# A hybrid attention and recurrence backbone on one core: the product of two norm vectors moves into the tile they are loaded into, and the pool of constants becomes 32 bytes shorter

## The chip, the core and the metric

The kernel runs on one core of a Trainium2 chip. A core has five engines that work side by side: TensorE (PE, with its weight loads shown apart as PEld), VectorE (DVE), ScalarE (ACT), GpSimd (POOL) and SyncE (SP). Here SP and POOL issue the DMAs. The metric is the device time of one execution in microseconds (us). The time before is the median of three runs.

## The reference

Two layers work on 1024 latent tokens of width 1024 (a raster 64 wide) with 256 context tokens before them. Layer 0 projects to neighbourhood attention with 16 heads and to a bidirectional mLSTM with 4 heads; layer 1 is a bidirectional gated linear attention (HGRN2) with 16 heads. Each has one input and one output projection. Cut to what the change touches:

```python
x, ctx: (1, 1024, 1024), (1, 256, 1024)            # float32 throughout
shift, scale, gate = split(silu(c) @ w_ada[l] + b_ada[l])
h = rms(x, norm_w[l]) * (1 + scale) + shift          # same for ctx
# layer 0
qa, ka, va, za, qb, kb, vb, ob, zb, g = split(h @ w_in_ab)
qa = rms(heads(qa, 16), q_norm)                      # q_norm, k_norm: 64 numbers each
ka = rms(heads(ka, 16), k_norm)
oa = softmax(qa * 64**-0.5 @ ka.T + bias) @ va       # neighbourhood 8 x 16, and the context
hb = mlstm_bidir(qb, kb, vb, gates)
x = x + gate * (concat(oa * silu(za), rms(hb * sigmoid(ob)) * silu(zb)) @ w_out_ab)
# layer 1
q, f_fwd, f_bwd, i, z = split(h @ w_in_c)
x = x + gate * ((rms(gla_bidir(silu(q), i, f)) * silu(z)) @ w_out_c)
```

Since a score is the product of a normed query and a normed key, the kernel multiplies q_norm, k_norm and 64**-0.5 = 0.125 into one vector, and applies it to the keys alone.

## The kernel before

**Precision.** The big products are done in three matmuls. A float32 operand is split into a high part, rounded to the matmul's own format (`fp32r` in the profile), and a low part, the rest: `split` (L73 on ACT, L74 on DVE). `dense` (L129, L130, L131) then adds high by high, high by low and low by high; `out_part` does the same for output projections (L858, L859, L860). In the names, `wh` and `wl` are a weight's two parts, `hh` and `hl` those of the modulated input h, `yh` and `yl` those of the mixers' output, `woh` and `wol` those of an output weight, `wzh` and `wzl` those of a weight of layer 1 that serves the value and gate columns. Smaller products (attention, recurrences, transposes) are plain float32.

Each matmul has a stationary operand, loaded into the array first (PEld), and a moving one, streamed through it. `proj_nat` has h stationary and a weight moving (256 or 512 columns); `proj_tr` has the weight stationary and h moving. In the profile's names the moving operand stands first.

**Stages.** Up to some 300 us: conditioning, norm and modulation of the input into `hh`, `hl`. Then layer 0 to about 1640 us: the attention (`na`), with the mLSTM's projections as filler between its steps, then the mLSTM's recurrence (`ml`), again with projections between. Then layer 0's output projection and layer 1's input (to about 1840 us), the 16 heads of layer 1 (`hg`, 88 us each), and from about 3290 us the last output projection, with blocks named w to w6 in the code.

**Order.** The order on each engine is set when the program is built, by a scheduler that works through the code and through priorities (`filler`, `urgent`). All waits are semaphores.

**Memory.** SBUF tiles have an address within a partition; each takes a multiple of 32 bytes. Pools of tiles grow from the left or, with `side="right"`, from the right end. The first pool on the left is the pool of constants, `const` (`cp` in the code, L1165), which starts at 16512. It holds ident (512 bytes), mhalf (32), ab0 and ab1 (128 each), cT and normw (64 each), badap (128), hnb (32), hnc (64), qkn (32), qknp (32), bg (32), lbc (128), sct (64), lb (128) and lbm (64): 1632 bytes, so that the next pool starts at 18144. All other pools on the left stand behind it: the weights of layer 0 (`w0`), the tiles of attention and recurrences (`na`, `ml`, `hg`), layer 1's wz, and the last projection's weights w3 to w6 (`wl1`). On the right stand a tile of 32 bytes (`edge`), then `hh` and `hl`, the weights of layer 1 (`w1`) and the y tiles of the last projection (`oy`).

The function that the diff touches is `build`; the lines that count are L1197 to L1201, where `qkn` is loaded by a DMA on POOL's queue and DVE makes the product `qknp`. That product is read by the attention's key preparation (`akh`, L686, and `akl`, L687).

Of the kernel before, what the change touches and what calls it, by code (L numbers as in the profile page):

```python
# [10 lines left out]
F32 = mybir.dt.float32  # L11
# [8 lines left out]
P = 128  # L20
# [25 lines left out]
class Prog:  # L46
# [1114 lines left out]
    def build(self):  # L1161
        tc, nc, a = self.tc, self.nc, self.a
        dma = nc.sync.dma_start
        with ExitStack() as es:
            cp = es.enter_context(tc.tile_pool(name="const", bufs=1))  # L1165
# [21 lines left out]
            def load(name, shape, eng=nc.gpsimd):  # L1187
                t = self.t(cp, shape, F32, name)
                eng.dma_start(out=t, in_=a[name])
                return t  # L1190
# [3 lines left out]
            self.badap = load("badap", [P, 2, 16])  # L1194
            self.hnb = load("hnb", [P, KD])
            self.hnc = load("hnc", [P, 16])
            qkn = load("qkn", [P, 2])  # L1197
            self.qkn = self.t(cp, [P, 1], F32, "qknp")
            nc.vector.tensor_scalar(
                out=self.qkn, in0=qkn[:, 0:1], scalar1=qkn[:, 1:2], scalar2=0.125, op0=ALU.mult, op1=ALU.mult  # L1200
            )  # L1201
# [10 lines left out]
            for i in range(2):  # L1212
# [6 lines left out]
                out=self.lb[:, 1, :], in0=self.lb[:, 0, :], scalar1=-1.0, scalar2=1.0, op0=ALU.mult, op1=ALU.add  # L1219
# [405 lines left out]
```

## Time and profile before

| | |
|---|---|
| median of three runs | 3446.57 us (3445.27 to 3448.31) |
| profiled execution | 3444.31 us |
| its span, first to last instruction | 3442.5 us |
| granted TensorE clock, mean | 0.992 |
| PE, PEld busy | 3368.1 us (98%), 2972.1 us (86%) |
| DVE, ACT, POOL busy | 2051.4, 1407.0, 664.0 us |
| DMA | 333.56 MB, mean 97 GB/s |

Busy time is the union of an engine's instructions. PE's matmuls overlap in a pipeline and their ends are modelled, so the pace of PE is read from the starts of matmuls that follow each other, not from their durations. Rows of a stage table give, for a stretch of time, the busy time of PE, PEld, DVE, ACT and POOL with the number of instructions, the granted clock (1.00 is full), the busy share of the DMA engines and GB/s. A row of a group gives line, engine, operation, names (out<-in), shape and count, then busy us, mean ns of one, and idle time ahead of it with what ended it. A row in order of time gives start and duration in us.

### The profile page before, as it was taken

What the parts mean: (1) busy time and instruction counts of PE and PEld (TensorE: products, weight loads), DVE (VectorE), ACT (ScalarE), POOL (GpSimd) and SP (SyncE); (2) the same over time, 40 slices, a digit from 0 to 9 for tenths busy, and PEclk for the clock granted to TensorE, in tenths of its full rate; (3) what the DMA queues carried; (4) which work ended last, traced back from release to release, by engine and by line L of the source; (5) the groups of instructions that cost most, each with busy time, mean ns of one, the idle gap of its engine ahead of it and who ended that gap; (6) DMA issues with size and microseconds to landing.
All of it is one profiled execution on the core that took longest, in us unless ns stands there. A gap on an engine that the chain in (4) does not pass through costs nothing.

```text
span 3442.5 us, 64358 instructions
## 1 busy us (share of the span) xinstructions
PE 3368.1 (98%) x25044; PEld 2972.1 (86%) x25044; DVE 2051.4 (60%) x4786; ACT 1407.0 (41%) x3310; POOL 664.0 (19%) x1036
## 2 busy tenths in 40 slices
PE   7999999999999999999999999999999999999988
PEld 5689999888989888898888999989999988889866
DVE  5336666566655466777666555555555555555657
ACT  5235544455444444454354333333333333333432
POOL 2121222122211111221100111111111111121023
PEclk9999999999999999999999999999999999999999
DMA  6522222232233443444652111111111111111364
GB/s 242 214 75 70 79 77 74 76 90 83 68 90 99 144 125 121 127 132 144 218 166 71 50 58 55 58 59 58 57 59 59 50 50 50 54 59 37 119 204 151
DMA packets 327152, 333.56 MB, mean 97 GB/s; under 512 B 30696, under 2 KB 277672, under 8 KB 324800
## 3 DMA queue, kind: packets, MB, share of 16 engines
q1 hardware_dynamic: 287808, 222.76, 21.8%
q0 software_dynamic: 39040, 106.69, 8.8%
q8 instruction: 197, 3.23, 0.4%
q14 instruction: 107, 0.88, 0.1%
HBM read 259.40 MB, written 69.79 MB: 96 GB/s over the span
## 4 chain that ended last, share of the span: by engine, by line
PE 87%; DMA 4%; issue 3%; DVE 3%; ACT 1%; POOL 1%; SPq 0%; POOLq 0%; DVEq 0%; ACTq 0%
PE mm L129 19%; PE mm L131 19%; PE mm L130 19%; PE s L1021 4%; PE acc L798 2%; PE tr L778 2%; PE mm L858 2%; PE mm L859 2%; PE mm L860 2%; PE s L579 2%; PE acc L570 2%; PE acc L560 1%; PE acc L1097 1%; PE tr L1033 1%; PE acc L1098 1%
## 5 line engine op out<-in xcount | busy, mean ns | idle before, releaser
L131 PE MATMUL mm<-hh,wl 128*128 128x512 f32 (+1 forms) x1600 | 584.2, 365 | 0.0
L129 PE MATMUL mm<-hh,wh 128*128 128x512 f32 (+1 forms) x1600 | 584.1, 365 | 0.0
L130 PE MATMUL mm<-hl,wh 128*128 128x512 f32 (+1 forms) x1600 | 583.6, 365 | 0.0
L129 PE MATMUL mm<-wh,hh 128*128 128x256 f32 (+1 forms) x1520 | 473.6, 312 | 1.7 <-ACT ev L314 1.0
L131 PE MATMUL mm<-wh,hl 128*128 128x256 f32 (+1 forms) x1520 | 470.1, 310 | 0.3 <-DVE hl L273 0.3
L130 PE MATMUL mm<-wl,hh 128*128 128x256 f32 (+1 forms) x1520 | 470.3, 309 | 0.0
L131 PEld LDWEIGHTS mm<-hh,wl 128*128 128x128 f32 x1600 | 301.6, 189 | 46.0 <-issue 0.3
L129 PEld LDWEIGHTS mm<-hh,wh 128*128 128x128 f32 x1600 | 301.9, 189 | 45.3 <-issue 0.8
L130 PEld LDWEIGHTS mm<-hl,wh 128*128 128x128 f32 x1600 | 301.8, 189 | 43.4 <-issue 0.2
L129 PEld LDWEIGHTS mm<-wh,hh 128*128 128x128 f32 x1520 | 286.3, 188 | 22.7 <-ACT ev L295 4.2
L131 PEld LDWEIGHTS mm<-wh,hl 128*128 128x128 f32 x1520 | 286.2, 188 | 13.5 <-issue 1.4
L130 PEld LDWEIGHTS mm<-wl,hh 128*128 128x128 f32 x1520 | 286.8, 189 | 12.5 <-issue 1.2
L129 PE MATMUL mm<-wzh,hh 128*128 128x256 f32 x1024 | 296.1, 289 | 0.6 <-ACT gEc L945 0.6
L131 PE MATMUL mm<-wzh,hl 128*128 128x256 f32 x1024 | 291.3, 284 | 0.0
L130 PE MATMUL mm<-wzl,hh 128*128 128x256 f32 x1024 | 290.5, 284 | 0.0
L74 DVE TENSOR_TENSOR wl<-wraw,wh 128x512 fp32r<-128x512 f32 x240 | 167.0, 700 | 175.4 <-ACT wh L73 172.1
L73 ACT CAST wh<-wraw 128x512 fp32r<-128x512 f32 x240 | 147.5, 619 | 243.4 <-PE mm L130 166.2
L129 PEld LDWEIGHTS mm<-wzh,hh 128*128 128x128 f32 x1024 | 193.5, 189 | 2.9 <-ACT gEc L945 0.8
L130 PEld LDWEIGHTS mm<-wzl,hh 128*128 128x128 f32 x1024 | 193.4, 189 | 1.7
L131 PEld LDWEIGHTS mm<-wzh,hl 128*128 128x128 f32 x1024 | 193.2, 189 | 1.2
L858 PE MATMUL mm<-woh,yh 128*128 128x512 f32 x422 | 169.8, 403 | 17.8 <-DVE og L1387 10.1
L1051 ACT COPY gksel<-gK 128x1024 f32<-128x1024 f32 x96 | 111.2, 1158 | 174.4 <-PE s L1021 128.9
(382 smaller groups left out, 7359.4 us busy)
## 6 DMA issues: line engine op xcount, KB each, us to landing
wraw<-in_wab_dram SPq DMA_DIRECT2D x112, 256.0 KB
wraw<-in_wc_dram SPq DMA_DIRECT2D x96, 256.0 KB
wraw<-yd SPq DMA_DIRECT2D x94, 256.0 KB
wraw<-in_wc_dram SPq DMA_DIRECT2D x128, 128.0 KB
md<-ev POOLq DMA_DIRECT2D x60, 256.0 KB, 2.7
mloz<-md SPq DMA_DIRECT2D x40, 256.0 KB
adar<-in_wada_dram SPq DMA_DIRECT2D x8, 1024.0 KB
adar<-in_wada_dram POOLq DMA_DIRECT2D x8, 1024.0 KB, 8.8
```

The lines of the kernel that those rows point to most:

```text
L73: nc.scalar.copy(hi, x)
L74: nc.vector.tensor_tensor(out=lo, in0=x, in1=hi.bitcast(F32), op=ALU.subtract)
L129: mm(ps, lhsT=lh(k), rhs=rh(k), start=(start and k == 0), stop=False)
L130: mm(ps, lhsT=lh(k), rhs=rl(k), start=False, stop=False)
L131: m = mm(ps, lhsT=ll(k), rhs=rh(k), start=False, stop=(stop and k == nk - 1))
L570: nc.tensor.matmul(num, lhsT=qc[:, j, :], rhs=C[d][:, j, :], start=False, stop=(j == 1))
L579: nc.tensor.matmul(u, lhsT=st["k"][c][:, j * P : (j + 1) * P], rhs=vw, start=True, stop=True)
L778: nc.tensor.transpose(pt[:nk, i, :], pr[:, o : o + nk], self.ident)
L798: m = nc.tensor.matmul(yp[h64], lhsT=v[:, h64], rhs=pTs[hd][:nk, i, :], start=(i == turn[0]), stop=(i == turn[-1]), tile_position=(0, hd * ...
L858: mm(ps, lhsT=yh[k], rhs=w.h(kk), start=(kk == 0), stop=False)
L1021: self.nc.tensor.matmul(out[s], lhsT=lhsT, rhs=rhs, start=True, stop=True, tile_position=(0, b * 64))
L1051: nc.scalar.copy(ksel.rearrange("p (b s i) -> p b s i", s=2, i=h), pick(K))
```

## The change

The tile `qkn` gets three columns. The DMA loads the two vectors into the first two, and the product is written to the third, in place of a tile of its own.

```diff
@@ -1194,8 +1194,9 @@
             self.badap = load("badap", [P, 2, 16])
             self.hnb = load("hnb", [P, KD])
             self.hnc = load("hnc", [P, 16])
-            qkn = load("qkn", [P, 2])
-            self.qkn = self.t(cp, [P, 1], F32, "qknp")
+            qkn = self.t(cp, [P, 3], F32, "qkn")
+            nc.gpsimd.dma_start(out=qkn[:, 0:2], in_=a["qkn"])
+            self.qkn = qkn[:, 2:3]
             nc.vector.tensor_scalar(
                 out=self.qkn, in0=qkn[:, 0:1], scalar1=qkn[:, 1:2], scalar2=0.125, op0=ALU.mult, op1=ALU.mult
             )
```

Three columns of float32 are 12 bytes and still take 32, so the pool of constants has one tile of 32 bytes fewer: 1600 bytes, and the next pool starts at 18112. In the built program every engine has the same instructions in the same order with the same waits; line numbers behind the edit grow by one. What differs is the name and place of the product, and the address of every left-side tile that comes after it, which is 32 lower. The places of the operands of the big products, as remainders:

| tile | side | address mod 512 before | after | mod 128 before | after |
|---|---|---|---|---|---|
| wh, wl of layer 0 | left | 288 | 256 | 32 | 0 |
| wxh, wxl of layer 0 | left | 288 or 352 | 256 or 320 | 32 or 96 | 0 or 64 |
| hh, hl | right | 448 | 448 | 64 | 64 |
| wh, wl of layer 1 | right | 448 | 448 | 64 | 64 |
| wzh, wzl of layer 1 | left | 224 | 192 | 96 | 64 |
| layer 0's output: woh, wol of its first block | right | 448 | 448 | 64 | 64 |
| its second block, and y beside it | left | 416, 160 | 384, 128 | 32, 32 | 0, 0 |
| last projection: y; weights of w5, w6, w3, w4 | right; left | 448; 224 | 448; 192 | 64; 96 | 64; 64 |

Within a tile, the slices that a matmul reads start at multiples of 512 bytes. The tiles of layer 1's recurrence (gv, gS, gQ) are 32 past a multiple of 64 before and multiples of 64 after; those of the attention's values (avc, avw) are the other way round; ident, in the pool of constants ahead of the edit, stays at a multiple of 128.

## The prediction

> **What bounds the kernel now.** I read the page first (busy shares, granted clock, chain), then busy time by stage, and then the order of time on PE alone, since the busy shares of a pipelined engine do not tell how far apart its matmuls stand.
>
> ```profile
> PE 3368.1 (98%) x25044; PEld 2972.1 (86%) x25044; DVE 2051.4 (60%) x4786; ACT 1407.0 (41%) x3310; POOL 664.0 (19%) x1036
> ...
> PE 87%; DMA 4%; issue 3%; DVE 3%; ACT 1%; POOL 1%; SPq 0%; POOLq 0%; DVEq 0%; ACTq 0%
> ...
> 0.00:100.00 100.00, 76.28 (x480) 54.07 (x481) 49.76 (x120) 52.09 (x111) 23.01 (x47) 0.91 0.68 251
> 300.00:1080.00 780.00, 780.00 (x6068) 704.98 (x6067) 484.82 (x1552) 381.51 (x1039) 171.87 (x236) 1.00 0.28 82
> 1720.00:3290.00 1570.00, 1552.95 (x13128) 1397.11 (x13127) 902.35 (x1523) 562.69 (x1188) 251.00 (x374) 1.00 0.21 65
> 3290.00:3442.00 152.00, 126.09 (x515) 98.11 (x513) 104.36 (x134) 48.16 (x88) 56.21 (x51) 0.92 0.62 194
> ```
>
> PE is busy for 98% of the span and makes 87% of the chain. In the stages of layer 0 (300:1080, 780 of 780 us) and of layer 1 (1720:3290, 1553 of 1570 us) it never rests, at a granted clock of 1.00. So a nanosecond more or less between two matmuls, in these two stages, goes straight into the span; only in the first 100 us and the last 152 us (PE 76 and 126 us busy) do other things, DMA above all, decide part of it.
>
> **What the change does.** It removes no work. The DMA of two columns, the multiplication of 128x1 and everything behind them stand in the same order on every engine, with the same waits. What it takes away is one tile of 32 bytes per partition, and with it every tile on the left side of SBUF that comes after the pool of constants lies 32 bytes lower, while hh, hl and all else on the right side stay. Call an address even if it is a multiple of 64 and odd if it is 32 past one. Before, the weights of layer 0 (wh, wl, wxh), the wz tiles of layer 1 and the last projection's weights (wl1) are odd, while hh, hl and y beside them are even; afterwards all of these are even. So the question is whether the place matters, and the trace has both kinds. The next rows are first and last of undisturbed runs on PE, in order of time: start, modelled duration, names (moving operand first, then the stationary one).
>
> ```profile
> 233.48 0.39 PE L129 MATMUL mm<-hh,wh 128*128 128x512 f32 x1
> ...
> 238.85 0.40 PE L131 MATMUL mm<-hh,wl 128*128 128x512 f32 x1
> ...
> 1864.07 0.39 PE L129 MATMUL mm<-hh,wh 128*128 128x512 f32 x1
> ...
> 1869.28 0.40 PE L131 MATMUL mm<-hh,wl 128*128 128x512 f32 x1
> ...
> 3428.90 0.40 PE L858 MATMUL mm<-woh,yh 128*128 128x512 f32 x1
> ...
> 3434.27 0.39 PE L860 MATMUL mm<-woh,yl 128*128 128x512 f32 x1
> ...
> 1759.26 0.39 PE L858 MATMUL mm<-woh,yh 128*128 128x512 f32 x1
> ...
> 1768.57 0.39 PE L860 MATMUL mm<-woh,yl 128*128 128x512 f32 x1
> ```
>
> The first three runs have 24 matmuls, the fourth 42. In the first, hh is even and wh odd: 5.37 us over 23 steps, 233.5 ns a step. In the second both are even: 5.21 us, 226.5 ns. In the third woh is odd and yh even: 5.37 us, 233.5 ns. In the fourth both are odd: 9.31 us over 41 steps, 227.1 ns. So for 512 columns it is not the place of one operand that costs, it is the two having unlike places, and it costs 7.0 ns. The distance of the tiles is no explanation: the second pair are both on the right, the fourth both on the left.
>
> [...]
>
> For 256 columns the rows say something else:
>
> ```profile
> 3124.40 0.28 PE L129 MATMUL mm<-wzh,hh 128*128 128x256 f32 x1
> ...
> 3127.08 0.28 PE L131 MATMUL mm<-wzh,hl 128*128 128x256 f32 x1
> ...
> 2604.72 0.28 PE L129 MATMUL mm<-hh,wh 128*128 128x256 f32 x1
> ...
> 2607.47 0.28 PE L131 MATMUL mm<-hh,wl 128*128 128x256 f32 x1
> ...
> 1129.73 0.28 PE L129 MATMUL mm<-wh,hh 128*128 128x256 f32 x1
> ...
> 1132.49 0.28 PE L131 MATMUL mm<-wh,hl 128*128 128x256 f32 x1
> ```
>
> Each run has 24 matmuls. In layer 1 the unlike pair (wz odd, hh even) takes 2.68 us over 23 steps, 116.5 ns; the like pair (hh and wh even) takes 2.75 us, 119.6 ns. In layer 0 the unlike pair (wh odd, hh even) takes 2.76 us, 120.0 ns. So at 256 columns likeness gains nothing, and may cost layer 1 3.1 ns a step. This speaks against the change.
>
> **How many there are.** Groups by form, the first six up to 1640 us, the next two from 1720 to 3290, the last from 3290 on; each stands for three lines (high by high, high by low, low by high).
>
> ```profile
> L129 PE MATMUL mm<-wh,hh 128*128 128x256 f32 x1280 | 373.3, 292 | 1.6 <-ACT ev L314 1.0 <-ACT hh L272 0.5
> ...
> L129 PE MATMUL mm<-hh,wh 128*128 128x512 f32 x384 | 152.6, 397 | 0.0
> ...
> L129 PE MATMUL mm<-wh,hh 128*128 128x512 f32 x240 | 100.3, 419 | 0.2 <-ACT wh L73 0.2
> ...
> L73 ACT CAST wh<-wraw 128x512 fp32r<-128x512 f32 x142 | 87.0, 618 | 78.3 <-DMA wraw<-in_wab_dram 47.1 <-PE mm L130 22.4 <-PE mm L131 5.1
> ...
> L129 PE MATMUL mm<-hh,wh 128*128 128x256 f32 x192 | 54.3, 283 | 0.0
> L129 PE MATMUL mm<-wxh,hh 128*128 128x512 f32 x80 | 32.6, 410 | 0.5 <-ACT wxh L73 0.5
> ...
> L129 PE MATMUL mm<-wzh,hh 128*128 128x256 f32 x1024 | 296.1, 289 | 0.6 <-ACT gEc L945 0.6
> ...
> L73 ACT CAST wh<-wraw 128x512 fp32r<-128x512 f32 x95 | 58.9, 620 | 153.7 <-PE mm L130 143.8 <-DMA wraw<-in_wc_dram 8.4 <-issue 1.3
> ...
> L858 PE MATMUL mm<-woh,yh 128*128 128x512 f32 x137 | 57.0, 416 | 12.5 <-DVE og L1387 10.1 <-ACT yh L73 2.2
> ```
>
> *512 columns, unlike now, like afterwards.* Layer 0 has 3 x (384 + 240 + 80) = 2112. At 7.0 ns that is 14.8 us at most. Its projections are cut by the attention's and the recurrence's own matmuls, and a run must settle first; I take two thirds, 9.9 us less (an estimate; bounds 0 and 14.8). Of the last 137 of L858, the four blocks w5, w6, w3, w4 make 4 x 4 x 8 = 128, with their three lines 384, in runs without a break: 2.7 us less.
>
> *256 columns.* Layer 1: 3 x 1024 = 3072. At 3.1 ns that is 9.5 us more at most, by two thirds 6.3 us more (bounds 0 and 9.5). Layer 0: 3 x 1280 = 3840, from 120.0 to 119.6, two thirds of 1.5 us: 1.0 us less. The 3 x 192 = 576 with hh moving: between 0 and 1.8 us more (3.1 ns each), I take 1.0.
>
> *Products in plain f32.* Both rows are from the chain, the groups from the whole span:
>
> ```profile
> 2542.00 0.87 PE tr L1033 x8
> ...
> 2573.25 0.45 PE s L1102 x4
> ...
> L1097 PE MATMUL acc<-gv,gA 128*128 128x128 f32 x256 | 51.1, 281 | 1.5 <-DVE gA L1117 1.2 <-ACT gA L1077 0.3
> ...
> L798 PE MATMUL acc<-apT,avc 128*64 128x128 f32 x640 | 49.7, 276 | 0.0
> L1098 PE MATMUL acc<-gS,gQ 128*128 128x128 f32 x256 | 49.4, 275 | 0.0
> L1099 PE MATMUL acc<-gS,gQ 128*128 128x128 f32 x256 | 49.3, 274 | 0.0
> ...
> L1102 PE MATMUL s<-gv,gkn 128*128 128x128 f32 x224 | 40.1, 274 | 0.0
> L1086 PE MATMUL s<-gv,gkn 128*128 128x128 f32 x224 | 39.3, 274 | 0.0
> ...
> L798 PE MATMUL acc<-apT,avw 96*64 96x128 f32 x384 | 33.5, 281 | 0.0
> ```
>
> With an even moving operand (ident) a transpose takes 0.87/8 = 109 ns, with an odd one (gv) a product takes 0.45/4 = 112. The five groups of layer 1 move gv or gS, odd now and even afterwards: 1216 x 3 = 3.6 us at most; since a transpose differs in more than the place, I take 2.4 less (bounds 0 and 3.6). In the attention avc and avw go from even to odd: 1024 rows, two side by side, 512 x 3 = 1.5 us more at most, I take 1.0.
>
> *The rest* costs nothing. ACT's casts take 618 ns with both tiles odd (layer 0) and 620 with wraw odd and wh even (layer 1), so it does not feel the place. The DMA engines are busy for 0.21 to 0.28 of the long stages, under a PE that is never idle; that cover is gone only in the first 100 us, where the destinations move from odd to even too. Without a row that separates them I put this at 0, between 1 us more and 1 less.
>
> Sum: -9.9 - 2.7 + 6.3 - 1.0 + 1.0 - 2.4 + 1.0 = -7.7 us. The profiled execution took 3444.3 us (span 3442.5), so 3436.6; it lies 2.3 us under the median of the runs shown, 3446.6, so the median should come to **3438.9**, 0.22% less.
>
> **Rivals.** (a) *The grid is 128 bytes, not 64; slower.* All like pairs in the trace are alike by 128 too (hh and wh of layer 1 both 64 past a multiple of 128, woh and yh of the fourth run both 32 past). Afterwards wz and the last projection's weights agree with hh and y by 128, but the weights of layer 0 are a multiple of 128 and hh is 64 past one. Then layer 1 pays its 9.5 us in full and the f32 products gain nothing, the last projection gains 2.7, layer 0 gains nothing, and the attention pays 1.5: +8.3, 3454.9. It decides as soon as layer 0's 512-wide steps stay above some 232 ns. The even step from 233.5 to 226.5 in four separate runs speaks for neither grid. (b) *The place is not the cause*; the unlike runs are slower for another reason, such as what runs beside them, and nothing moves: 3446.6. Against it: runs three and four have the same code and no other stage's work between. (c) *More is gained.* Layer 0's 256-wide steps come down from 120.0 to the 116.5 that layer 1 shows, 3840 x 3.5 = 13.4 us at most, two thirds 9, in place of 1.0: 3430.9; with full shares at 512 as well, 3426.
>
> **Chances.** Forecast 0.53, (a) 0.20, (b) 0.13, (c) 0.14. What can be told from no change here is about 0.2%, or 7 us. The forecast's own range is 3432 to 3444: two thirds of it lies beyond 0.2%, one third within. Faster is then 0.36 + 0.14 and a little from layer 1's cost staying out: 0.54; same 0.17 + 0.13 less that little: 0.27; slower 0.19. The range for 8 in 10 reaches from 3425, where (c) ends, to 3454, most of (a).
>
> **What would show it.** Right: the runs of layer 0 at 512 columns (as at 233 us) step by 227 ns, and the last projection's too; wz's runs in layer 1 step by 119 to 120; the head of layer 1 takes some 0.3 us longer and layer 0 ends about 10 us sooner. Wrong: layer 0 steps by 232 or more (then a), all steps as before (b), or wz's step stays at 116.5 or layer 0's 256-wide ones fall to 117 (c). Counts, waits and the order of rows should be the same in both profiles.

## The result, and the profile after

The changed kernel takes 3438.65 us (median of 13 runs, 3434.49 to 3442.60), the kernel before 3443.89 beside it (13 runs). The ratio is 0.9983, 95% interval 0.9975 to 0.9992: faster, by about 5 us. The profiled execution took 3438.97 us, 5.3 less than that of before, and its span 3437.2 us, 5.3 less.

The page and the stage table of the changed kernel:

```profile
PE 3364.1 (98%) x25044; PEld 2972.0 (86%) x25044; DVE 2050.0 (60%) x4786; ACT 1404.6 (41%) x3310; POOL 662.3 (19%) x1036
...
PE 87%; DMA 4%; issue 3%; DVE 3%; ACT 1%; POOL 1%; SPq 0%; POOLq 0%; DVEq 0%; ACTq 0%
...
300.00:1080.00 780.00, 780.00 (x6124) 705.18 (x6123) 486.03 (x1564) 383.27 (x1046) 171.12 (x235) 1.00 0.29 82
1720.00:3290.00 1570.00, 1554.87 (x13115) 1400.93 (x13114) 898.24 (x1517) 557.33 (x1181) 251.46 (x375) 1.00 0.21 64
```

Each engine has as many instructions as before, and PE has the same 87% of the chain. What differs is the pace. In the stretch of layer 0 PE starts 6124 matmuls where it started 6068, in that of layer 1 13115 where it started 13128. Layer 0 has become quicker; that layer 1 is slower is only a hint here, since its work now begins earlier within the same stretch, and the steps below decide it.

The same runs as in the prediction, in order of time (first and last matmul of each):

```profile
231.09 0.40 PE L129 MATMUL mm<-hh,wh 128*128 128x512 f32 x1
...
236.46 0.39 PE L131 MATMUL mm<-hh,wl 128*128 128x512 f32 x1
...
124.00 0.40 PE L130 MATMUL mm<-wl,hh 128*128 128x512 f32 x1
...
127.68 0.39 PE L131 MATMUL mm<-wh,hl 128*128 128x512 f32 x1
...
1120.01 0.28 PE L129 MATMUL mm<-wh,hh 128*128 128x256 f32 x1
...
1122.72 0.28 PE L131 MATMUL mm<-wh,hl 128*128 128x256 f32 x1
...
3130.36 0.28 PE L129 MATMUL mm<-wzh,hh 128*128 128x256 f32 x1
...
3133.12 0.28 PE L131 MATMUL mm<-wzh,hl 128*128 128x256 f32 x1
...
3423.73 0.39 PE L858 MATMUL mm<-woh,yh 128*128 128x512 f32 x1
...
3428.94 0.39 PE L860 MATMUL mm<-woh,yl 128*128 128x512 f32 x1
...
1854.31 0.39 PE L129 MATMUL mm<-hh,wh 128*128 128x512 f32 x1
...
2598.85 0.28 PE L129 MATMUL mm<-hh,wh 128*128 128x256 f32 x1
...
2687.22 0.28 PE L129 MATMUL mm<-hh,wh 128*128 128x256 f32 x1
```

Layer 0 with h moving, 512 columns (24 matmuls): 5.37 us over 23 steps, 233.5 ns, as before. Layer 0 with the weight moving, 512 columns (17 matmuls): 3.68 us over 16 steps, 230.0 ns. Layer 0 with the weight moving, 256 columns (24): 2.71 over 23, 117.8 ns, where it was 120.0. Layer 1's wz (24): 2.76 over 23, 120.0 ns, where it was 116.5. Last projection (24): 5.21 over 23, 226.5, where it was 233.5. The first run of layer 1 starts at 1854.31, 9.8 us sooner than the 1864.07 of before. A head of layer 1, from the first to the second of the last two rows, takes 88.37 us. Two runs of before that the prediction did not show, for comparison:

```profile
125.14 0.40 PE L130 MATMUL mm<-wl,hh 128*128 128x512 f32 x1
...
128.88 0.39 PE L131 MATMUL mm<-wh,hl 128*128 128x512 f32 x1
...
2692.80 0.28 PE L129 MATMUL mm<-hh,wh 128*128 128x256 f32 x1
```

With the weight moving, layer 0's 512-wide run took 3.74 us over 16 steps, 233.8 ns; a head of layer 1 took 2692.80 - 2604.72 = 88.08 us, 0.29 less than now.

A run can mislead, so here are the means over all undisturbed steps of a kind (the distance between the starts of two big products, up to 145 ns at 256 columns and 260 ns at 512, so that interrupted ones are left out), and what count times difference makes:

| steps | count | before, ns | after, ns | us |
|---|---|---|---|---|
| layer 0, 512, h moving | 1020 | 234.08 | 233.20 | -0.9 |
| layer 0, 512, w moving | 600 | 233.42 | 229.82 | -2.2 |
| layer 0, 512, wx moving | 127 | 233.41 | 230.10 | -0.4 |
| layer 0, 256, w moving | 3083 | 119.71 | 117.47 | -6.9 |
| layer 0, 256, h moving | 496 | 118.00 | 115.27 | -1.4 |
| layer 1, 256, wz moving | 2675 | 116.81 | 119.47 | +7.1 |
| layer 1, 256, h moving (over wz 291 of them) | 960 | 119.01 | 119.43 | +0.4 |
| last projection, 512, w3 to w6 | 350 | 233.28 | 227.31 | -2.1 |

The sum is -6.4 us, and the span lost 5.3. By stage, layer 1's first wz product starts at 1863.79 us instead of 1873.53, 9.7 sooner; from its first to its last wz product layer 1 takes 1357.1 us instead of 1351.8, 5.2 more, where the steps say 7.5; and what follows is 0.8 shorter. So the time went the way PE's steps say, stage by stage, though in layer 1 some of it did not reach the span, and not by the amounts that were forecast. One row of the table fits no notion of even and odd at all: layer 0's 512-wide steps with h moving kept their 233 ns although both operands are now on multiples of 64.

### The profile page after: what moved, and what is told of

The parts are those of the page before. It is cut to its first block, busy times and chain, and to the rows that moved or that the text cites. A ratio compares the mean times of both kernels' runs of the same rounds, so it can differ in the third digit from the quotient of the medians.

```text
span 3437.2 us, 64358 instructions
## 1 busy us (share of the span) xinstructions
PE 3364.1 (98%) x25044; PEld 2972.0 (86%) x25044; DVE 2050.0 (60%) x4786; ACT 1404.6 (41%) x3310; POOL 662.3 (19%) x1036
## 4 chain that ended last, share of the span: by engine, by line
PE 87%; DMA 4%; issue 3%; DVE 3%; ACT 1%; POOL 1%; SPq 0%; POOLq 0%; DVEq 0%; ACTq 0%
PE mm L129 19%; PE mm L131 19%; PE mm L130 19%; PE s L1021 4%; PE acc L798 2%; PE tr L778 2%; PE mm L858 2%; PE mm L859 2%; PE mm L860 2%; PE s L579 2%; PE acc L570 2%; PE acc L1097 1%; PE acc L560 1%; PE tr L1033 1%; PE acc L1098 1%
```

## Experiments

Below, d is the address of a product's moving operand less that of its stationary one, modulo 256 bytes. When the experiments began it was only a suspicion that a difference counts (theory R, then with a period of 128 bytes) and not the place of the left-side tiles as such (theory A).

**The step by itself.** A kernel of fp32r products alone, with the moving and the stationary operand shifted by 0, 32, 64 and 96 bytes (letters a to d). The base of the moving tile was a multiple of 256, that of the stationary one 128 past it, so d = 128 + 32 x (letter of m - letter of s). It computes none of the reference.

```diff
+for n, w in ((512, "h"), (256, "q"), (128, "o")):
+    for i in range(4):
+        for j in range(4):
+            run(f"{w}m{'abcd'[i]}s{'abcd'[j]}", mov, sta, n, 8 * i, 8 * j)   # 48 products each
```

> A kernel of its own that measures nothing but the step between matmuls: 48 matmuls in a row, each with a new stationary operand, for every pair of places of the moving operand (0, 32, 64, 96 bytes past a multiple of 128) and of the stationary one, at 512, 256 and 128 columns of fp32r, and 24 in a row of plain f32 at 256 and 128 columns. It computes none of the reference. Theory R (relative place): the step depends on the offset of moving against stationary within 128 bytes and on the width, not on the place of either alone, so the 16 pairs of a width fall into 4 groups. Offset 0: 226.7 ns at 512 and 120 ns at 256. Offset 64: 230 to 233 and 114 to 118. Offsets 32 and 96: 233.5 and 116.7 to 120. Theory A (absolute place): the step depends on whether an operand starts on a multiple of 64 or 128, so pairs with the same offset differ (0 and 0 fast at 512, 32 and 32 slow). For plain f32 both expect no step to move by over 1 ns, as in the two profiles.

At 512 columns shifting both by the same amount left 232.2 to 233.5 ns; the only pairs under 232 were hmasc and hmbsd, 228.9 ns, both d = 64. At 256 columns the steps went from 113.3 to 120.0 with d. At 128 columns fp32r steps were 111.7 ns for all pairs. Plain float32 was 215.8 ns at 256 columns and 111.7 at 128 for all five pairs of places tried (differences 96 to 224). The traces of before and after say the same of the small float32 products in the kernel: undisturbed steps with gS moving over gQ are 111.06 and 110.91 ns, gv over gkn 110.26 and 110.16, gv over gA 111.25 and 111.24, gv over gknc 111.68 and 110.96. There both operands move together, so their difference stays; in the transposes ident stays and the other operand moves, and they step by 108.99 and 108.93 (over aP), 108.91 and 109.13 (over gK). So there is an effect at 256 and 512 columns of fp32r, it goes by the difference, and nothing shows that the small float32 products have a part in it. That 226.7 ns did not occur at all spoke against a period of 128: the pairs alike by 128 bytes stood at 232.2 to 233.5.

**Only the place, without the edit.** The kernel before, with a tile of 32 bytes added to the pool of constants, so that the left side moves up by 32 and not down.

```diff
+            nc.vector.memset(self.t(cp, [P, 8], F32, "padc"), 0.0)
```

> The kernel before with a pool of constants of 1664 bytes in place of 1632 (one more tile of 32 bytes): the left side moves up by 32 bytes, where the change moves it down. Layer 0's weights then have offset 0 to h, layer 1's wz and the last projection's weights offset 64. Theory R: layer 0's 512-wide runs step by 226.7 (10.1 us less in all), its 256-wide ones stay at 119.5 to 120 (0.1 more), wz's step becomes 117.5 (1.8 more), with h moving over wz 1.2 less, the last projection steps by 229.8 (1.2 less): 10.6 us less, ratio to before 0.997, faster than the change. Theory A (what counts is that left-side tiles start on multiples of 64): the same as the changed kernel, 0.9985, with wz at 119.5 and layer 0's 512-wide runs with h moving at 233.

**The other side.** The kernel before, with the tile at the right edge 64 bytes long instead of 32, so that the whole right side moves down by 32. Every d is as in the run above; every address of the operands is another.

```diff
-            nc.vector.memset(self.t(edge, [P, 8], F32, "edge"), 0.0)
+            nc.vector.memset(self.t(edge, [P, 16], F32, "edge"), 0.0)
```

> The kernel before with the right-side tile edge 64 bytes long in place of 32: the left side stays where it was before, and the right side moves down by 32 bytes. All offsets of weights to h are those of the kernel with the pool of 1664 bytes, but every operand of them lies 32 bytes lower (h 32 past a multiple of 128 in place of 64). Theory R: the same time as that kernel within 2 us, ratio to before 0.997, and the same steps. Theory A: not that time; with no operand of the big products on a multiple of 64 nothing is gained, 0.999 to 1.002.

The first took 3438.79 us, ratio 0.9985 (0.9976 to 0.9994), the second 3440.46, ratio 0.9989 (0.9980 to 0.9998). They agree within 1.7 us. The order of time on PE, first and last of 24 matmuls, of the first and then of the second:

```profile
232.62 0.39 PE L129 MATMUL mm<-hh,wh 128*128 128x512 f32 x1
...
237.97 0.39 PE L131 MATMUL mm<-hh,wl 128*128 128x512 f32 x1
...
1125.98 0.28 PE L129 MATMUL mm<-wh,hh 128*128 128x256 f32 x1
...
1128.70 0.28 PE L131 MATMUL mm<-wh,hl 128*128 128x256 f32 x1
...
3132.67 0.28 PE L129 MATMUL mm<-wzh,hh 128*128 128x256 f32 x1
...
3135.38 0.28 PE L131 MATMUL mm<-wzh,hl 128*128 128x256 f32 x1
```

```profile
232.84 0.39 PE L129 MATMUL mm<-hh,wh 128*128 128x512 f32 x1
...
238.18 0.39 PE L131 MATMUL mm<-hh,wl 128*128 128x512 f32 x1
...
1126.85 0.28 PE L129 MATMUL mm<-wh,hh 128*128 128x256 f32 x1
...
1129.57 0.28 PE L131 MATMUL mm<-wh,hl 128*128 128x256 f32 x1
...
3132.91 0.28 PE L129 MATMUL mm<-wzh,hh 128*128 128x256 f32 x1
...
3135.61 0.28 PE L131 MATMUL mm<-wzh,hl 128*128 128x256 f32 x1
```

Over 23 steps each: 5.35 and 5.34 us, 2.72 and 2.72, 2.71 and 2.70. The means over all steps agree within 0.3 ns in every kind (table below). So the side does not matter, nor the place of either operand: the difference does. But layer 0's 512-wide steps, expected at about 227 with d = 128, are at 232.6 and 232.2 in these runs: theory R with a period of 128 missed its 0.997, and the first run's ratio came out at theory A's 0.9985. That ratio alone would have spoken for the wrong theory; the steps decided, with wz at 117.6 and not at A's 119.5, and the second run, for which A had asked 0.999 to 1.002 (0.9989 measured), with the same steps.

**Layer 1 put back.** The changed kernel with 32 bytes at the front of layer 1's pool, so that wz lies where it lay before and all else stays changed.

```diff
+                nc.vector.memset(self.t(pool, [P, 8], F32, "padh", 1), 0.0)
```

> The changed kernel with a tile of 32 bytes at the front of layer 1's pool hg: layer 1's tiles, wz among them, are back at their addresses of before, all else stays as changed. If wz's step of 119.5 in place of 116.8 is what the change costs (2670 back-to-back steps by 2.7 ns, 7.1 us, and 0.2 us with h moving): 7 us faster than the changed kernel, ratio to before 0.9963. If the heads of layer 1 are longer in the changed kernel for another reason: no faster than the changed kernel, 0.9985.

3431.43 us, ratio 0.9962 (0.9948 to 0.9975). Taking back layer 1's part gains 7.2 us on the changed kernel (0.0021 in the ratios, whose intervals meet at 0.9975), close to its +7.1. In the traces, though, only 4.4 us lie in layer 1 itself, which takes 1352.6 us from its first to its last wz product where the changed kernel takes 1357.1; so that the two figures agree so closely is in part chance.

**The place put back.** The changed kernel, with its new load, and 32 bytes of padding in the pool of constants.

```diff
+            nc.vector.memset(self.t(cp, [P, 8], F32, "padc"), 0.0)
```

> The changed kernel with 32 bytes of padding put back into the pool of constants: the new load of the norm vectors stays, every later tile on the left lies where it lay before. Theory place (all of the difference comes from where later tiles lie): ratio to the kernel before 1.000, between 0.9990 and 1.0010; steps of layer 0's 256-wide products back at 119.7 ns, of layer 1's gate products at 116.8. Rival (the third column itself saves the time): 0.998, as the change measured.

3444.41 us, ratio 1.0002 (0.9994 to 1.0011). Its runs in layer 0 and layer 1:

```profile
1130.33 0.28 PE L129 MATMUL mm<-wh,hh 128*128 128x256 f32 x1
...
1133.09 0.28 PE L131 MATMUL mm<-wh,hl 128*128 128x256 f32 x1
...
3138.74 0.28 PE L129 MATMUL mm<-wzh,hh 128*128 128x256 f32 x1
...
3141.43 0.28 PE L131 MATMUL mm<-wzh,hl 128*128 128x256 f32 x1
```

2.76 and 2.69 us over 23 steps, as before the change. The third column by itself is worth nothing that can be measured; what the change gains comes from the place of the later tiles.

**The whole period.** Products alone again (none of the reference), d from 0 to 480 bytes in steps of 32 (letters a to p), 96 products each, with the stationary operand at its base (sa) and 64 bytes past it (sc). In the built program both bases lie 128 past a multiple of 512, not on one as the text below has it; the differences are as said.

> Computes none of the reference: runs of 96 fp32r products, each with a new stationary operand, the moving operand 0 to 480 bytes ahead of the stationary one in steps of 32 (letters a to p), at 512 and 256 columns, once with the stationary operand on a multiple of 512 bytes (sa) and once 64 bytes past it (sc). Theory R256 (the step goes by the difference of the two addresses mod 256): at 512 columns letters eight apart agree within 0.5 ns; the differences 0, 256 give 227 and 64, 320 give 229, all others 232 to 235; with the stationary operand moved by 64 bytes the same list shifts by two letters. Theory R512 (period 512): letters eight apart differ, 227 once in sixteen. Theory A (the moving operand's place alone): moving the stationary operand changes nothing. At 256 columns: difference 192 at 113 to 118, 0 and 96 at 119 to 120, the rest between 117 and 120.

The groups of some tiles: shortest, median and longest modelled duration in ns, then the first and the last start in us, which are 95 steps apart.

```profile
L37 PE MATMUL hmasa<-mov,sta x96: 389/389/389, 36.3 to 57.8; 128*128 128x512 f32 x96
L37 PE MATMUL hmbsa<-mov,sta x96: 393/396/399, 58.1 to 80.2; 128*128 128x512 f32 x96
L37 PE MATMUL hmcsa<-mov,sta x96: 388/392/398, 80.5 to 102.2; 128*128 128x512 f32 x96
L37 PE MATMUL hmisa<-mov,sta x96: 389/389/395, 214.5 to 236.1; 128*128 128x512 f32 x96
L37 PE MATMUL hmasc<-mov,sta x96: 394/394/399, 392.8 to 414.9; 128*128 128x512 f32 x96
L37 PE MATMUL hmcsc<-mov,sta x96: 389/389/398, 437.6 to 459.1; 128*128 128x512 f32 x96
L37 PE MATMUL qmasa<-mov,sta x96: 279/283/283, 749.2 to 760.6; 128*128 128x256 f32 x96
L37 PE MATMUL qmgsa<-mov,sta x96: 276/276/286, 817.5 to 828.3; 128*128 128x256 f32 x96
```

With d = 0 (hmasa, and with both operands shifted hmcsc) 95 steps take 21.5 us, 226.3 ns a step; with 32 (hmbsa) 22.1, 232.6; with 64 (hmcsa) 21.7, 228.4; with 192 (hmasc, the stationary operand alone shifted) 22.1; a difference of 256 bytes (hmisa) is as good as 0 (21.6, to the tenth that the row gives). At 256 columns d = 0 (qmasa) takes 11.4 us, 120.0 ns, and 192 (qmgsa) 10.8, 113.7. From the starts themselves, over the last two thirds of each run:

| d | 0 | 32 | 64 | 96 | 128 | 160 | 192 | 224 |
|---|---|---|---|---|---|---|---|---|
| 512 columns, ns | 226.7 | 233.3 | 228.9 | 233.4 | 233.3 | 234.3 | 233.3 | 233.3 |
| 256 columns, ns | 120.0 | 117.8 | 117.8 | 120.0 | 118.7 | 117.4 | 113.3 | 118.3 |

Letters eight apart agree within 0.1 ns, and so do all pairs of equal d with the stationary operand shifted. So theory R256 is right, in steps of 32 bytes as far as tried: the period is 256 bytes, not 512, and moving the stationary operand does change the step. What is best at 512 columns (0) is, with 96, worst at 256.

**Three kernels built on the table.** First the changed kernel with 192 bytes at the front of layer 1's pool: wz at d = 192.

```diff
+                nc.vector.memset(self.t(pool, [P, 48], F32, "padh", 1), 0.0)
```

> The changed kernel with 192 bytes of padding at the front of layer 1's pool, so that its gate weights lie 192 bytes past the stationary operand mod 256, where the change has them 0 and the kernel before 32. Theory R256: 2670 steps at 113.3 to 117.8 ns (what the products at 192 measured) in place of 119.5, so 4.5 to 16.6 us less than the change: 3422 to 3434 us, ratio 0.9935 to 0.997. Theory A (a place 32 past a multiple of 64 is what counts): places stay on multiples of 64, 3438.7, ratio 0.9983.

3422.45 us, ratio 0.9937 (0.9923 to 0.9950). A run of wz:

```profile
3114.27 0.28 PE L129 MATMUL mm<-wzh,hh 128*128 128x256 f32 x1
...
3116.88 0.28 PE L131 MATMUL mm<-wzh,hl 128*128 128x256 f32 x1
```

2.61 us over 23 steps, 113.5 ns; the mean over all is 114.65, 4.8 less than in the changed kernel. 2675 x 4.8 = 12.9 us, and a little from h over wz. The changed kernel's ratio falls with this padding by 0.0046, 16 us; in the traces layer 1, from its first to its last wz product, is 11.9 us shorter (1345.2 for 1357.1). The other 4 us are within what the two intervals leave open; no steps show them.

Then layer 0's weights at d = 192 too:

```diff
+            nc.vector.memset(self.t(cp, [P, 32], F32, "padc", 1), 0.0)
...
+                nc.vector.memset(self.t(pool, [P, 16], F32, "padh", 1), 0.0)
...
+                nc.vector.memset(self.t(wl1, [P, 32], F32, "pado", 1), 0.0)
```

> The changed kernel with 128 bytes more in the pool of constants, 64 in layer 1's pool and 128 ahead of the last projection's weights: layer 0's weights 192 past its activations (64 before them as moving operand), layer 1's gate weights 192 past, the last projection's still 0. Theory R256, against the change: layer 0's 512-wide w products +3.5 ns x 760 = +2.7 us, h products -4.2 x 1025 = -4.3, 256-wide w products 113.3 to 117.8 in place of 117.5, x 3083 = -12.9 to +1.0, h products 117.6 in place of 115.3, x 496 = +1.2; layer 1 -16.6 to -4.5. Sum -30 to -4: 3409 to 3435 us, ratio 0.990 to 0.997. Theory A (all of these places are multiples of 64): as the change, 3438.7, ratio 0.9983.

3418.57 us, ratio 0.9922 (0.9909 to 0.9936): faster than the kernel before by 0.8% and than the changed one by 0.6%. Layer 0, the weight moving at 256 columns and h at 512:

```profile
230.46 0.39 PE L129 MATMUL mm<-hh,wh 128*128 128x512 f32 x1
...
235.73 0.39 PE L131 MATMUL mm<-hh,wl 128*128 128x512 f32 x1
...
1112.62 0.28 PE L129 MATMUL mm<-wh,hh 128*128 128x256 f32 x1
...
1115.22 0.28 PE L131 MATMUL mm<-wh,hl 128*128 128x256 f32 x1
```

5.27 us over 23 steps, 229.1 ns (d = 64), and 2.60 over 23, 113.0 (d = 192). The mean of these 256-wide steps is 115.3: some runs keep a second rhythm at the same d, such as this one of 24 matmuls, 2.71 us over 23 steps, 117.8 ns:

```profile
1123.75 0.28 PE L129 MATMUL mm<-wh,hh 128*128 128x256 f32 x1
...
1126.46 0.28 PE L131 MATMUL mm<-wh,hl 128*128 128x256 f32 x1
```

Against the run above layer 0 should gain some 6 us by its steps. In the traces the first wz product starts 4.2 us sooner (1854.26 for 1858.44), but the spans differ by only 1.8 and the medians by 3.9. With intervals that overlap this last bit is not shown by the times.

Last, layer 0 as the prediction had imagined the change: weights and h at equal remainders, d = 0, with wz still at 192 and the last projection at 192.

```diff
+            nc.vector.memset(self.t(cp, [P, 48], F32, "padc"), 0.0)
```

> The changed kernel with 192 bytes more in the pool of constants: layer 0's weights then lie at the same remainder as its activations (difference 0 mod 256, what the prediction took the change to do), layer 1's gate weights at 192 as in the run with 192 bytes of padding in layer 1's pool, the last projection's at 192. Theory R256, against that run (3422.45): layer 0's 512-wide steps at about 227.5, -2.3 x 760 = -1.7 us for w and -5.7 x 1025 = -5.8 for h moving; its 256-wide steps at about 119.6, +2.3 x 3083 = +7.1 and +4.3 x 496 = +2.1; the last projection at 233.3, +6.1 x 360 = +2.2. Sum +3.9: 3426, ratio 0.9947. Rival (the prediction's own sizes, 7.0 ns at 512 columns and nothing at 256): -12 from layer 0, 3412.

Ratio 0.9950 (0.9937 to 0.9964), 3428.21 us beside 3447.43 for the kernel before. A 256-wide run of layer 0:

```profile
1123.82 0.28 PE L129 MATMUL mm<-wh,hh 128*128 128x256 f32 x1
...
1126.58 0.28 PE L131 MATMUL mm<-wh,hl 128*128 128x256 f32 x1
```

2.76 us over 23 steps, 120.0 ns. The 512-wide steps do fall, to 228.2 with h moving and 229.4 with the weight, but the 256-wide ones, three times as many, rise to 119.5, so that against the run with wz at 192 alone layer 0 loses 3.5 us by its steps, and the last projection 2.2. The ratio is 0.0013 above that run's, 4.5 us; the intervals overlap, so the times alone do not show a loss. They do rule out the rival's 12 us less (3412 us), as do the 256-wide steps.

**Whose stationary operand?** In the traces a product's weight load starts about 0.2 us ahead of it, close to one step (for howna below, the loads start from 103.4 to 125.4 us and the products from 103.6 to 125.6), so it stands beside the product before. Products alone once more (none of the reference), with places that alternate so that d is constant either to a product's own stationary operand ("own") or to the next one's ("next"), and with one stationary operand for all 96 ("one").

```diff
+run(w + "owna", n, (0, 8), (0, 8))      # moving, stationary: shift in floats of even and odd products
+run(w + "nexta", n, (8, 0), (0, 8))
+run(w + "onea", n, (0, 0), (0, 0), True)
+run(w + "oneb", n, (8, 8), (0, 0), True)
```

> Computes none of the reference: runs of 96 fp32r products at 512 (h) and 256 (q) columns. plaina, plainb, plaing: moving operand 0, 32 and 192 bytes ahead of every stationary one: 226.7, 233.3, 233.3 ns at 512 and 120.0, 117.8, 113.3 at 256, as in the run before. owna, owng: the places alternate so that the difference to the product's own stationary operand is always 0 or always 192, and to the next one's 32 and 224, or 64. nexta, nextg: the difference to the next one's is always 0 or always 192, to the own one's 32 and 224, or 64. Theory N (the weights loaded beside a product are the next one's, so the difference to the next counts): hnexta 226.7, howna 233.3; hnextg 233.3, howng 229; qnexta 120.0, qowna about 118; qnextg 113.3, qowng 117.8. Theory O (the product's own): each pair the other way round. onea, oneb, oneg: one and the same stationary operand 96 times; if the effect lies in the weight load these differ by place like the plain ones wherever the weights are loaded anew, and are alike if they are not.

```profile
L37 PE MATMUL howna<-mov,sta x96: 389/395/405, 103.6 to 125.6; 128*128 128x512 f32 x96
L37 PE MATMUL hnexta<-mov,sta x96: 388/394/398, 125.9 to 147.9; 128*128 128x512 f32 x96
L37 PE MATMUL honea<-mov,sta x96: 389/389/400, 192.6 to 214.2; 128*128 128x512 f32 x96
L37 PE MATMUL honeb<-mov,sta x96: 393/396/399, 214.4 to 236.6; 128*128 128x512 f32 x96
```

howna and hnexta both take 22.0 us over 95 steps, 231.7 ns by their starts: neither theory's 226.7 or 233.3. The other pair at 512 columns, hnextg at 233.3 and howng at 230.0, comes within 1 ns of what the next one's difference asks for (233.3 and 229), and so do qnexta at 120.0 and qowna at 118.7 (120.0 and about 118); but qowng and qnextg are both 116.7, where it asks for 117.8 and 113.3. So theory O, the product's own operand alone, fits no pair, and theory N fits two of four: whose stationary operand it is stays open. Using one stationary operand for all products changes nothing (226.7 at d = 0, 233.3 at 32), and the trace still shows 96 weight loads for each of those runs.

All kernels in one table; each cell has d and the mean of all undisturbed steps in ns:

| kernel | layer 0, 256, w | layer 0, 256, h | layer 0, 512, w | layer 0, 512, h | layer 1, wz | last projection | ratio |
|---|---|---|---|---|---|---|---|
| before | 96: 119.7 | 160: 118.0 | 96: 233.4 | 160: 234.1 | 32: 116.8 | 32: 233.3 | 1 |
| after | 64: 117.5 | 192: 115.3 | 64: 229.8 | 192: 233.2 | 0: 119.5 | 0: 227.3 | 0.9983 |
| left side up 32 | 128: 118.8 | 128: 118.9 | 128: 232.4 | 128: 232.7 | 64: 117.6 | 64: 229.2 | 0.9985 |
| right side down 32 | 128: 118.9 | 128: 118.9 | 128: 232.5 | 128: 232.8 | 64: 117.7 | 64: 229.0 | 0.9989 |
| after, place put back | 96: 119.7 | 160: 118.0 | 96: 233.5 | 160: 234.1 | 32: 116.8 | 32: 233.4 | 1.0002 |
| after, layer 1 put back | 64: 117.5 | 192: 115.3 | 64: 229.9 | 192: 233.2 | 32: 116.8 | 0: 227.3 | 0.9962 |
| after, wz at 192 | 64: 117.3 | 192: 115.3 | 64: 229.8 | 192: 233.2 | 192: 114.7 | 0: 227.2 | 0.9937 |
| layer 0 at 192 too | 192: 115.3 | 64: 117.0 | 192: 233.2 | 64: 229.6 | 192: 114.7 | 0: 227.1 | 0.9922 |
| layer 0 at 0 | 0: 119.5 | 0: 119.4 | 0: 229.4 | 0: 228.2 | 192: 114.7 | 192: 233.3 | 0.9950 |

The whole kernels follow the table of products alone in the main, but not to the nanosecond: at 512 columns layer 0's means at d = 0 are 228.2 and 229.4 where the products alone have 226.7, and at 256 columns wz's mean at d = 32 is 116.8 where they have 117.8, and those at d = 192 are 114.7 to 115.3 where they have 113.3. Why is open.

## Why the prediction was right, and where it was not

The total was right: 3438.9 forecast, 3438.65 measured, well inside the range, and "faster" as forecast. Right were also that work and order do not change, that the place of the later tiles is the cause (the run with the place put back, 1.0002), and that it is the place of two operands relative to each other (the two runs that move one side alone, and the products alone). That PE's steps go straight into the span was right in the main: -6.4 us by steps, -5.3 in the span. The terms of the sum are another matter.

- *Layer 0 at 512 columns, -9.9: failed.* It measured about -3.5. The two thirds allowed for runs that settle first, and the trace of before has such runs: in layer 1, 512 columns with h moving (d = 0), undisturbed steps take 224 to 236 ns up to the ninth of a run and 226 to 227 from the tenth on. The step that failed is the one that called places even and odd by 64 bytes. The four runs it was read from had d = 160 and 32 (unlike) and d = 0 (both like ones); that 0 was equality modulo 256 could not be seen from them, because no run had operands that were both even and apart. The change put layer 0 at d = 64 (w moving) and 192 (h moving), where a step takes 229.8 and 233.2 ns, not 226.5. The kernel with layer 0 at d = 0 has 228.2 and 229.4, so even there the 7.0 ns would have been 4.0 to 5.9.
- *Layer 0 at 256 columns, -1.0 for w moving and +1.0 for the 576 products with h moving: failed.* It measured -6.9 and -1.4. The forecast had one like pair at 119.6 and took it for all of them. This is the mechanism of rival (c), "layer 0's 256-wide steps come down", at two thirds of its step: 2.2 ns less, not 3.5.
- *Layer 1's wz, +6.3: right.* +7.1 by its steps, with 2.66 ns a step (3.1 forecast) on 87% of the products, not two thirds; +5.2 in the stage. Here the change did bring d = 0.
- *Last projection, -2.7: right but for size.* -2.1, with 6.0 ns a step.
- *Plain float32, -2.4 and +1.0: failed, nothing of them was found.* The products alone do not change with the places tried, and the steps with gS and gv moving, which the change took from odd to even, still take 110 to 111 ns (figures above); their differences times their counts make 0.2 us. The step that failed is the one that put 109 against 112 ns, a transpose against a product, down to the place of the moving operand.
- *Rival (a), a grid of 128.* Its sign, that layer 0's 512-wide steps stay above some 232 ns, came true for h moving alone (233.2). The grid is 256, so neither the forecast's 64 nor the rival's 128; with d = 128 the steps are 232.4.
- *Rival (b), the place is not the cause:* refuted by the two runs that move the left side or the right side alone.

Of the signs that were named, wz at 119 to 120, the last projection at 227, the head some 0.3 us longer (0.29) and layer 0 ending about 10 us sooner (9.8, by the first run of layer 1) came true; layer 0's 512-wide steps at 227 did not. Two of the signs of being wrong came true instead: layer 0's 512-wide steps at 232 or more, with h moving (233.2), and its 256-wide ones near 117 (117.5). In layer 0 the 6.4 us that were missing at 512 columns are outweighed by the 8.3 that came unforeseen at 256; the 1.4 us that float32 did not give, the 0.6 of the last projection and the 1.2 of layer 1 go the other way, and together they bring the sum from -7.7 to -6.4. The median was met more closely than that because the sum was made against 3446.6, while the kernel before came to 3443.89 over 13 runs. So the closeness of the total is luck for the most part: the costs of wz and the gain of the last projection were forecast, but layer 0's gain came from other products than the forecast had it from.

## What to carry to other kernels

Where PE is the bound, an edit that only shortens a pool can move the time, because it moves every later tile (here the ratio was 0.9983, and 1.0002 with the places put back): before a small gain is put down to an edit, put the old addresses back with padding and measure. When a pace seems to go by place, vary both operands over a whole period in a kernel of that operation alone before giving the rule a grid; a few pairs from a trace fit several grids. Then lay the costly products out by the table, each width by its own row, since the best place at 512 columns is among the worst at 256 (d = 0: 226.7 and 120.0 ns), and measure again: the whole kernels here differ from the table by up to 3 ns a step.

## What the runs showed of the hardware

- The step between fp32r matmuls that follow each other goes by the difference of moving and stationary address modulo 256 bytes (tried in steps of 32): 226.7 to 234.3 ns at 512 columns, 113.3 to 120.0 at 256. At 128 columns it is 111.6 to 111.7 ns at every difference tried (32 to 224). Plain float32 steps by 215.8 ns at 256 columns and 111.7 at 128 at every difference tried (96 to 224).
- The difference has a sign: 64 and 192 are the same distance and take 228.9 and 233.3 ns at 512 columns, 117.8 and 113.3 at 256.
- At 256 columns there are two rhythms for some differences: 118.7 and 120.0 ns for 128, 117.3 and 120.0 for 160, 113.3 and 117.8 for 192, all in the first run of products alone (120.0 at 128 in qmasa, 113.3 and 117.8 at 192 in qmcsa and qmdsb). A whole kernel has two as well (runs of 113.0 and 117.8 ns with layer 0 at 192). What chooses between them is open.
- With places that alternate, steps of 231.7 ns at 512 columns and 116.7 at 256 fit neither the difference to a product's own stationary operand nor that to the next one's. Why the difference counts at all is open; no run here shows it.
